# A PEER decoder block: the last gathered chunk's v rows summed on VectorE, some u row products held behind the gate expansion

## The chip, the core and the metric

The kernel runs on one core of one Trainium2 chip. Times are device microseconds (us) of one execution. A core has TensorE (PE in the rows), VectorE (DVE), ScalarE (ACT), GpSimd (POOL) and SyncE (SP), each with its own queue of instructions worked off in order, and 16 DMA engines.

## What is computed

A hybrid block over 1024 tokens plus 16 meta tokens of width 1024: a convolution and a latent attention in parallel, a projection, and then the part that the change touches, an expert mixer with 16384 experts. Per token and head, 16 experts are picked out of 128 x 128 pairs of keys, so 128 experts per token:

```python
        eidx = jnp.take_along_axis(cidx..., sel, axis=-1)
        g = jax.nn.softmax(top_s, axis=-1)
        u = u_tab[eidx]
        act = jax.nn.gelu(jnp.einsum('chkd,cd->chk', u, xb).astype(jnp.float32), approximate=False)
        w = (g * act).astype(xb.dtype)
        return jnp.einsum('chk,chkd->cd', w, v_tab[eidx])
```

The block's input is added, and a last RMS norm gives the output.

## The kernel before, in words

The tokens go in eight chunks of 128. The mixer has two ways of working. Chunks 4 to 7 (DENSE) go through all 16384 experts: `expand` (L741) spreads the gates of a chunk into a full table in DRAM, `g_d`; then `dense` (L801) goes over the 128 first keys i1, in 32 groups of four. For each i1, `dense_u` (L789) multiplies a 128-expert piece of u by the 512 tokens (24 matmuls of 128x512, `pa`), ScalarE takes the Gelu, VectorE multiplies by the gates (L820) and splits the product into a high and a low part (L823, L824); per group the weighted v pieces are summed (96 matmuls, `pv`) and VectorE adds them to `acc` (L837), eight additions per group, 256 in all. Every loaded weight is split into high and low parts by ScalarE and VectorE (L785, L786).

Chunks 0 to 3 (GATHER) fetch only the rows they need. `gather_u` (L679) takes 128 steps j; at each, GpSimd issues an indirect DMA (L690) that brings one u row of 1024 floats per token (512 KB), and VectorE forms the products with the token and their sum (L693, one column of `dots`). Four buffers `ug` hold such rows. When all 128 are there, Gelu and gates make the weights (L695, L696). `gather_v` (L698) then goes by tokens differently: each indirect DMA (L716) brings the 128 v rows of one token, with the experts on the partitions (hence the transposed indices `eT` of `turn`, L659, and the transposed weights), and TensorE sums them over the partitions with 32-column matmuls (L720, 16 for four tokens). Eight buffers `vg` hold such rows.

`gather_all` (L729) chains these: u of chunk 0; then v of chunk 0 beside u of chunk 1; v1 beside u2; v2 beside u3; v3. `dense` takes 1.1 such steps per i1, each of 8 or of 4 rows. This is the order in which the program is written; a scheduler then places the instructions of every engine by its own model, with the written order as priority, so row products of chunk 1 stand as early as the gate expansion, and those of chunk 2 and 3 all along the dense loop. One `xn` buffer serves all chunks, so u1, u2, u3 and what follows them stand in a row.

The expansion of a chunk has four rounds of four passes. A pass makes four VectorE tables of 128x1024 (L755 `two`, L756 `one`, L757 `ah`, L758 `al`; every second `al` is GpSimd's), 16 matmuls, and four ScalarE copies into `st` (L766). A round ends with two stores of 1 MB to `g_d` (L770); three `st` buffers serve two per round, so a round's second half waits for the first store of the round before. The dense loop's first gate load, `gt` (L814), waits for the last rounds' stores.

At the end `finish` (L736) norms each chunk: a ScalarE square and sum (L148), two GpSimd operations (L140, L141), a VectorE product (L738), the store (L739).

Of the kernel before, what the change touches and what calls it, by code (L numbers as in the profile page):

```python
# [4 lines left out]

# [8 lines left out]
F32 = mybir.dt.float32  # L14
# [6 lines left out]
OP = mybir.AluOpType  # L21
# [4 lines left out]
P = 128  # L26
D = 1024
# [35 lines left out]
GATHER = [0, 1, 2, 3]  # L63
# [12 lines left out]
ALP = [1, 3]  # L76
GEB = 6
VB = 8
UB = (4, 3)


@with_exitstack
def trunk_kernel(ctx, tc, x, meta, g_mix, w_ab, w_lat, g_q, w_uq, g_kv, w_ukv, conv_w, conv_b,
                 g_ln, b_ln, g_out, w_out, g_ffn, wq, keys, u_tab, v_tab, u_t, g_fin, cs, out):
    nc = tc.nc
    V, A, G, PE = nc.vector, nc.scalar, nc.gpsimd, nc.tensor
# [16 lines left out]
    h_d = [dram.tile([P, D], F32, name=f"h_d{c}") for c in range(NC)]  # L103
# [25 lines left out]
    def load_bcast(t, ap):  # L129
        nc.sync.dma_start(t, bass.AP(tensor=ap.tensor, offset=ap.offset, ap=[[0, P], [1, t.shape[-1]]]))  # L130
        return t
# [23 lines left out]
    def transpose_to(dst, src, m):  # L155
        PE.transpose(dst, src, ident[:m, :m])
# [448 lines left out]
        V.max_index(i[:, 8:16], v[:, 8:16], s)  # L605

    chunks = [None] * NC
    MTs, tops, weights, picks, kbds = {}, {}, {}, {}, {}

    def select(c, sv, sx):  # L610
# [47 lines left out]

    def turn(c):  # L659

        ef, g = picks[c]
        tp = bank(f"et{c}", (P, 4, P), "s" if c in DENSE else "c")
        transpose_to(tp[:, 0], ef, P)
        eT = const.tile([P, P], I32, name=f"eT{c}", tag="eT", bufs=5)
        V.tensor_copy(eT, tp[:, 0])
        if c in GATHER:
            chunks[c] += (eT,)
        else:
            transpose_to(tp[:, 1], g.rearrange("p h k -> p (h k)"), P)
            t = sel.tile([P, 4, P], F16, name=f"gd{c}", tag="gd", bufs=len(DENSE))  # L670
            A.activation(t[:, 0], tp[:, 1], AF.Copy, scale=GSCALE)
            V.scalar_tensor_tensor(t[:, 1], tp[:, 1], GSCALE, t[:, 0], op0=OP.mult, op1=OP.subtract)
            ii = sel.tile([P, 2, P], I32, name=f"ii{c}", tag="ii", bufs=1)
            V.tensor_scalar(ii[:, 0], eT, 7, None, op0=OP.logical_shift_right)
            V.tensor_scalar(ii[:, 1], eT, NK - 1, None, op0=OP.bitwise_and)
            V.tensor_copy(t[:, 2:4], ii)
            chunks[c] = t

    def gather_u(c):  # L679

        g, ei = chunks[c][:2]
        xn = gu.tile([P, D], F32, name=f"xn{c}", tag="xn", bufs=1)
        nc.sync.dma_start(xn, xn_d[c])
        dots = gu.tile([P, P], F32, name=f"dots{c}", tag="dots", bufs=2)
        weights[c] = dots
        for j in range(P):
            if j and j % 4 == 0:
                yield
            ug = gu.tile([P, D], F32, name=f"ug{c}_{j}", tag="ug", bufs=4)
            G.indirect_dma_start(out=ug, out_offset=None, in_=u_tab,  # L690
                                 in_offset=bass.IndirectOffsetOnAxis(ap=ei[:, j:j + 1], axis=0))
            junk = gu.tile([P, D], BF, name="ujunk", tag="ujunk", bufs=1)
            V.scalar_tensor_tensor(junk, ug, 1.0, xn, op0=OP.mult, op1=OP.mult, accum_out=dots[:, j:j + 1])  # L693
        yield
        A.activation(dots, dots, AF.Gelu)  # L695
        V.tensor_tensor(dots, dots, g.rearrange("p h k -> p (h k)"), op=OP.mult)  # L696

    def gather_v(c):  # L698

# [6 lines left out]
        for q in range(4):  # L706
# [4 lines left out]
            for i in range(8):  # L711
                vg = []
                for j in range(4):
                    t = 32 * j + 8 * q + i
                    vg.append(gp.tile([P, D], F32, name=f"vg{c}_{t}", tag="vg", bufs=VB))
                    G.indirect_dma_start(out=vg[j], out_offset=None, in_=v_tab,  # L716
# [6 lines left out]
                yield  # L723
        ht = gp.tile([P, D], F32, name=f"ht{c}", tag="vg", bufs=VB)
        nc.sync.dma_start(ht, h_d[c])
        V.tensor_tensor(ht, ht, acc, op=OP.add)
        finish(c, ht, load_bcast(gp.tile([P, D], F32, name=f"gfin{c}", tag="vg", bufs=VB), g_fin))

    def gather_all():  # L729
        streams = [gather_u(GATHER[0])]  # L730
        for k in range(len(GATHER) + 1):
            for _ in itertools.zip_longest(*streams):
                yield
            streams = [gather_v(c) for c in GATHER[k:k + 1]] + [gather_u(c) for c in GATHER[k + 1:k + 2]]

    def finish(c, ht, gfin):  # L736
        r = inv_rms(ht, f"o{c}")
        V.scalar_tensor_tensor(ht, ht, r, gfin, op0=OP.mult, op1=OP.mult)  # L738
        nc.scalar.dma_start(out[c * P:(c + 1) * P], ht)  # L739

    def expand(ci):  # L741

        c = DENSE[ci]
        t = chunks[c]
        for q in range(P // TG):
            st = [ex.tile([P, NK // 2, TG], F32, name=f"st{c}_{q}_{i}", tag="st", bufs=STB) for i in range(2)]
            for r0 in range(0, TG, TH):
                sh = [P, TH // 2, NK, 2]

                def col(r):  # L750
                    cv = t[:, r, q * TG + r0:q * TG + r0 + TH].rearrange("p (a b) -> p a b", b=2)
                    return cv[:, :, None, :].broadcast_to(sh)
                one, two, ah, al = [ex.tile(sh, F16, name=f"{n}{c}_{q}_{r0}", tag=n, bufs=b)
                                    for n, b in (("one", 1), ("two", 2), ("ah", 2), ("al", 2))]
                V.tensor_tensor(two, io[:, None].broadcast_to(sh), col(3), op=OP.is_equal)  # L755
                V.tensor_tensor(one, io[:, None].broadcast_to(sh), col(2), op=OP.is_equal)  # L756
                V.tensor_tensor(ah, one, col(0), op=OP.mult)  # L757
                (G if r0 // TH in ALP else V).tensor_tensor(al, one, col(1), op=OP.mult)  # L758
                for r in range(0, TH, 4):
                    pg = bank(f"pg{c}_{q}_{r0}_{r}", (P, 4, NK), "bs"[r // 4 % 2])  # L760
                    for k in range(4):
                        a, b = divmod(r + k, 2)
                        PE.matmul(pg[:, k], two[:, a, :, b], ah[:, a, :, b], start=True, stop=False)  # L763
                        PE.matmul(pg[:, k], two[:, a, :, b], al[:, a, :, b], start=False, stop=True)  # L764
                    for i in range(2):
                        A.activation(st[i][:, :, r0 + r:r0 + r + 4].rearrange("p a b -> p b a"),  # L766
                                     pg[:, :, i * NK // 2:(i + 1) * NK // 2], AF.Copy, scale=1.0 / GSCALE)
            for i in range(2):
                gs = slice(i * NK // 2 // NG, (i + 1) * NK // 2 // NG)
                nc.sync.dma_start(g_d[gs, :, ci * (P // TG) + q].rearrange("g p r -> p g r"),  # L770
                                  st[i].rearrange("p (g a) t -> p g (a t)", a=NG))
# [94 lines left out]
    gu = ctx.enter_context(tc.tile_pool(name="gu", bufs=1, side="right", **RW))  # L866
# [19 lines left out]
    gp = ctx.enter_context(tc.tile_pool(name="gp", bufs=1, side="right", **RW))  # L886
# [98 lines left out]
```

## Time and profile before

| what | value |
|---|---|
| time, median of 3 runs | 3013.92 us (3005.61 to 3018.28) |
| the profiled execution: its own time | 2999.61 us |
| its span, first to last instruction | 2997.8 us |
| busy TensorE, VectorE, ScalarE, GpSimd | 86%, 72%, 34%, 53% |
| mean granted TensorE clock | 0.91 of full speed |
| DMA | 860.44 MB, mean 287 GB/s |

The shares of the whole span mix three kinds of stage, so the rows below are read by stage: the last seven rounds of the gate expansion (1255 to 1391 us from the span's start), the dense loop (first addition to `acc` at 1437, last at 2989), and in it the stretch in which chunk 3's v rows are summed (2626 to 2902). The profiled execution is a little shorter than any of the three timed ones.

### The profile page before, as it was taken

The page shows a single profiled execution, that of the slowest core. Times are in us where ns is not written, and L with a number is a line of the kernel's source. Part 1 is how long each engine was busy: PE and PEld are TensorE (multiplying, and loading weights), DVE is VectorE, ACT ScalarE, POOL GpSimd, SP SyncE. Part 2 cuts the span into 40 slices and gives each one's busy share as a digit, 9 for nine tenths or more (in the row PEclk, how much of TensorE's full clock was granted, in tenths as well). Part 3 has the DMA queues.
Part 4 walks back from the last instruction along what each step waited for, and adds up shares of the span by engine and source line. Part 5 has one row for each costly group of instructions (what it writes and reads, how often), then busy time and mean ns, then how long its engine had stood idle before and what let it go on. Part 6 is the DMA issues. An engine that isn't in the chain of part 4 may idle for free. (4 is left out here: it accounts for less than half of the span.)

```text
span 2997.8 us, 40243 instructions
## 1 busy us (share of the span) xinstructions
PE 2577.1 (86%) x13295; PEld 1932.0 (64%) x13295; DVE 2156.3 (72%) x4749; ACT 1005.9 (34%) x2200; POOL 1579.9 (53%) x1524
## 2 busy tenths in 40 slices
PE   6778758888894764744999999999999999999998
PEld 6675537766662443533887767777777777666666
DVE  4888866999988789997998866565666665533344
ACT  5435425353440332342332223232322222222222
POOL 5885463544658767654344554544454545344420
PEclk9988858998997887856999999999999999999999
DMA  4114789898896998888899999999998989799972
GB/s 141 48 50 129 229 271 318 301 306 285 281 332 233 385 322 272 264 279 306 309 322 318 340 381 340 346 329 344 352 344 329 358 317 362 277 338 332 331 286 74
DMA packets 373138, 860.44 MB, mean 287 GB/s; under 512 B 38016, under 2 KB 134464, under 8 KB 368832
## 3 DMA queue, kind: packets, MB, share of 16 engines
q0 software_dynamic: 147456, 536.94, 50.2%
q1 hardware_dynamic: 217104, 297.77, 29.4%
q10 hardware_dynamic: 8368, 23.15, 2.2%
q8 instruction: 105, 1.72, 0.2%
q14 instruction: 105, 0.86, 0.1%
HBM read 801.02 MB, written 56.71 MB: 286 GB/s over the span
## 5 line engine op out<-in xcount | busy, mean ns | idle before, releaser
L690 POOL DMA_INDIRECT ug<-in_dram,ei x512 | 580.8, 1134 | 662.9 <-DVE ujunk L693 450.9
L716 POOL DMA_INDIRECT vg<-in_dram,eT x512 | 555.6, 1085 | 469.6 <-PE gv L720 332.3
L693 DVE SCALAR_TENSOR_TENSOR ujunk<-ug,xn 128x1024 bf16<-128x1024 f32 x512 | 651.1, 1272 | 70.2 <-DMA ug<-in_dram,ei 67.8
L837 DVE TENSOR_TENSOR acc<-acc,pv 128x512 f32<-128x512 f32 x256 | 171.5, 685 | 251.3 <-PE pv L178 250.8
L720 PE MATMUL gv<-vg,wd 128*32 128x512 f32 x2048 | 266.4, 635 | 12.8 <-DMA vg<-in_dram,eT 12.8
L178 PE MATMUL pv<-v_0h,wh 128*128 128x512 f32 x512 | 201.9, 397 | 18.6 <-ACT wh L823 14.1
L178 PE MATMUL pa<-xdh,u_1l 128*128 128x512 f32 x512 | 203.3, 397 | 5.5 <-DVE u_1l L786 5.5
L178 PE MATMUL pa<-xdh,u_1h 128*128 128x512 f32 x512 | 202.8, 396 | 0.7 <-ACT u_1h L785 0.7
L178 PE MATMUL pa<-xdh,u_0h 128*128 128x512 f32 x512 | 202.4, 395 | 0.8 <-ACT u_0h L785 0.8
L178 PE MATMUL pa<-xdl,u_0h 128*128 128x512 f32 x512 | 201.8, 394 | 0.0
L178 PE MATMUL pa<-xdl,u_1h 128*128 128x512 f32 x512 | 201.7, 394 | 0.0
L178 PE MATMUL pa<-xdh,u_0l 128*128 128x512 f32 x512 | 201.3, 393 | 0.0
L178 PE MATMUL pv<-v_0l,wh 128*128 128x512 f32 x512 | 199.3, 392 | 0.0
L178 PE MATMUL pv<-v_1l,wh 128*128 128x512 f32 x512 | 199.2, 392 | 0.0
L178 PE MATMUL pv<-v_1h,wl 128*128 128x512 f32 x512 | 199.1, 391 | 0.0
L785 ACT ACTIVATE u_1h<-u_1r 128x512 fp32r<-128x512 f32 x128 | 80.7, 631 | 352.5 <-PE pa L178 336.3
L178 PE MATMUL pv<-v_1h,wh 128*128 128x512 f32 x512 | 195.7, 394 | 0.0
L178 PE MATMUL pv<-v_0h,wl 128*128 128x512 f32 x512 | 194.6, 393 | 0.0
L763 PE MATMUL pg<-ah,two 128*128 128x128 f16 x512 | 96.3, 269 | 114.0 <-DVE ah L757 80.6
L766 ACT ACTIVATE st<-pg 128x256 f32<-128x256 f32 x256 | 128.7, 649 | 158.2 <-PE pg L764 122.6
L785 ACT ACTIVATE u_0h<-u_0r 128x512 fp32r<-128x512 f32 x128 | 80.5, 629 | 262.1 <-PE pa L178 251.4
L786 DVE TENSOR_TENSOR u_0l<-u_0r,u_0h 128x512 fp32r<-128x512 f32 x128 | 89.7, 701 | 94.2 <-ACT u_0h L785 89.6
(449 smaller groups left out, 5844.3 us busy)
## 6 DMA issues: line engine op xcount, KB each, us to landing
g_d<-st SPq DMA_DIRECT2D x32, 1024.0 KB
u_0r<-in_dram SPq DMA_DIRECT2D x128, 256.0 KB
u_1r<-in_dram SPq DMA_DIRECT2D x128, 256.0 KB
gt<-g_d SPq DMA_DIRECT2D x32, 1024.0 KB
v_0r<-in_dram SPq DMA_DIRECT2D x128, 256.0 KB
v_1r<-in_dram SPq DMA_DIRECT2D x128, 256.0 KB
wo<-in_dram SPq DMA_DIRECT2D x80, 256.0 KB
wq<-in_dram SPq DMA_DIRECT2D x80, 256.0 KB
```

What stands on the lines that cost most here:

```text
L178: PE.matmul(dst, l, r, start=first and j == 0, stop=last and j == 2)
L690: G.indirect_dma_start(out=ug, out_offset=None, in_=u_tab, in_offset=bass.IndirectOffsetOnAxis(ap=ei[:, j:j + 1], axis=0))
L693: V.scalar_tensor_tensor(junk, ug, 1.0, xn, op0=OP.mult, op1=OP.mult, accum_out=dots[:, j:j + 1])
L716: G.indirect_dma_start(out=vg[j], out_offset=None, in_=v_tab, in_offset=bass.IndirectOffsetOnAxis(ap=eT[:, t:t + 1], axis=0))
L720: PE.matmul(acc[32 * j:32 * j + 32, 512 * n:512 * n + 512], w[:, j, 32 * i:32 * i + 32], vg[j][:, 512 * n:512 * n + 512], start=q == 0 and ...
L763: PE.matmul(pg[:, k], two[:, a, :, b], ah[:, a, :, b], start=True, stop=False)
L766: A.activation(st[i][:, :, r0 + r:r0 + r + 4].rearrange("p a b -> p b a"), pg[:, :, i * NK // 2:(i + 1) * NK // 2], AF.Copy, scale=1.0 / G ...
L785: A.activation(hi, raw, AF.Copy)
L786: V.tensor_tensor(lo, raw, hi.bitcast(F32), op=OP.subtract)
L837: V.tensor_tensor(a, a, pv, op=OP.add)
```

## The change

For the chunks in VROWS (chunk 3) v is gathered as u is: step j brings each token's own j-th v row to its partition, and VectorE multiplies it by the token's weight and adds it to `ht`, which starts as the block's input. The transposed indices, the transposed weights and 512 matmuls of chunk 3 fall away. `ht` takes the `xn` buffer. And the row products of chunk 1 from step 72 on are put behind the last `ah` of the whole expansion in VectorE's queue (`issue_after`).

```diff
+UHOLD = 72
+VROWS = [3]
 def turn(c):
+        if c in VROWS:
+            return
 def gather_u(c):
-            V.scalar_tensor_tensor(junk, ug, 1.0, xn, op0=OP.mult, op1=OP.mult, accum_out=dots[:, j:j + 1])
+            with tc.issue_after(expanded[-1]) if c == GATHER[1] and j >= UHOLD else nullcontext():
+                V.scalar_tensor_tensor(junk, ug, 1.0, xn, op0=OP.mult, op1=OP.mult, accum_out=dots[:, j:j + 1])
+    def gather_v_rows(c):
+        ei = chunks[c][1]
+        ht = gu.tile([P, D], F32, name=f"ht{c}", tag="xn", bufs=1)
+        nc.sync.dma_start(ht, h_d[c])
+        for j in range(P):
+            vg = gp.tile([P, D], F32, name=f"vg{c}_{j}", tag="vg", bufs=VB)
+            G.indirect_dma_start(out=vg, out_offset=None, in_=v_tab,
+                                 in_offset=bass.IndirectOffsetOnAxis(ap=ei[:, j:j + 1], axis=0))
+            V.scalar_tensor_tensor(ht, vg, weights[c][:, j:j + 1], ht, op0=OP.mult, op1=OP.add)
+            if j % 4 == 3:
+                yield
+        finish(c, ht, load_bcast(gp.tile([P, D], F32, name=f"gfin{c}", tag="vg", bufs=VB), g_fin))
 def gather_all():
-            streams = [gather_v(c) for c in GATHER[k:k + 1]] + [gather_u(c) for c in GATHER[k + 1:k + 2]]
+            streams = [(gather_v_rows if c in VROWS else gather_v)(c) for c in GATHER[k:k + 1]] + [gather_u(c) for c in GATHER[k + 1:k + 2]]
 def expand(ci):
-                V.tensor_tensor(ah, one, col(0), op=OP.mult)
+                expanded.append(V.tensor_tensor(ah, one, col(0), op=OP.mult).ins)
```

How the instructions stand after it is shown at three places. First VectorE's queue in the second round of the third chunk's expansion (`ujunk` is a row product of chunk 1, its step is the number behind `ug`; `two`, `one`, `ah`, `al` are the expansion's tables). Before:

```order
L757 TENSOR_TENSOR ah_1_0_9971<-one_1_0_9969,gd_9824 128x1024
L758 TENSOR_TENSOR al_1_0_9972<-one_1_0_9969,gd_9824 128x1024
L756 TENSOR_TENSOR one_1_8_9999<-io,gd_9824 128x1024
L757 TENSOR_TENSOR ah_1_8_10001<-one_1_8_9999,gd_9824 128x1024
L693 SCALAR_TENSOR_TENSOR ujunk,dots_11703<-ug_73_13444,xn_11701 128x1024
L693 SCALAR_TENSOR_TENSOR ujunk,dots_11703<-ug_74_13448,xn_11701 128x1024
L756 TENSOR_TENSOR one_1_16_10029<-io,gd_9824 128x1024
```

With the change (its lines are numbered 21 higher here):

```order
L778 TENSOR_TENSOR ah_1_0_9967<-one_1_0_9965,gd_9820 128x1024
L779 TENSOR_TENSOR al_1_0_9968<-one_1_0_9965,gd_9820 128x1024
L776 TENSOR_TENSOR two_1_8_9996<-io,gd_9820 128x1024
L777 TENSOR_TENSOR one_1_8_9995<-io,gd_9820 128x1024
L778 TENSOR_TENSOR ah_1_8_9997<-one_1_8_9995,gd_9820 128x1024
L776 TENSOR_TENSOR two_1_16_10026<-io,gd_9820 128x1024
```

No row product stands among the last 28 of the 64 passes any more, where 38 stood (steps 72 to 109). The second place is VectorE's queue where the expansion ends, with the change:

```order
L778 TENSOR_TENSOR ah_3_24_10873<-one_3_24_10871,gd_9832 128x1024
L700 SCALAR_TENSOR_TENSOR ujunk,dots_11699<-ug_72_13436,xn_11697 128x1024
L700 SCALAR_TENSOR_TENSOR ujunk,dots_11699<-ug_73_13440,xn_11697 128x1024
L700 SCALAR_TENSOR_TENSOR ujunk,dots_11699<-ug_74_13444,xn_11697 128x1024
L700 SCALAR_TENSOR_TENSOR ujunk,dots_11699<-ug_75_13448,xn_11697 128x1024
```

The held products start here; step 127 of chunk 1 now stands behind 27 of the 256 additions to `acc` (before: behind 7), step 127 of chunk 3 behind 216 (before: 191). The third place is the end of VectorE's queue. Before (`v_3_1l` is a split, `acc<-acc,pv` an addition of the dense loop, the last rows the norms):

```order
L786 TENSOR_TENSOR v_3_1l<-v_3_1r,v_3_1h 128x512
L837 TENSOR_TENSOR acc<-acc,pv_1_0_25895 128x512
L837 TENSOR_TENSOR acc<-acc,pv_1_1_25909 128x512
L837 TENSOR_TENSOR acc<-acc,pv_1_2_25923 128x512
L738 SCALAR_TENSOR_TENSOR acc<-acc,os_25954,gfin 128x1024
L738 SCALAR_TENSOR_TENSOR acc<-acc,os_25961,gfin 128x1024
L837 TENSOR_TENSOR acc<-acc,pv_1_3_25937 128x512
L738 SCALAR_TENSOR_TENSOR acc<-acc,os_25968,gfin 128x1024
```

With the change (`ht<-vg` sums a v row of chunk 3):

```order
L858 TENSOR_TENSOR acc<-acc,pv_1_0_25749 128x512
L714 SCALAR_TENSOR_TENSOR ht_21870<-vg_80_23714,dots_18431,ht_21870 128x1024
L858 TENSOR_TENSOR acc<-acc,pv_1_1_25763 128x512
L858 TENSOR_TENSOR acc<-acc,pv_1_2_25777 128x512
L714 SCALAR_TENSOR_TENSOR ht_21870<-vg_81_23717,dots_18431,ht_21870 128x1024
L858 TENSOR_TENSOR acc<-acc,pv_1_3_25791 128x512
L714 SCALAR_TENSOR_TENSOR ht_21870<-vg_82_23720,dots_18431,ht_21870 128x1024
L714 SCALAR_TENSOR_TENSOR ht_21870<-vg_83_23723,dots_18431,ht_21870 128x1024
```

Of the 128 v rows of chunk 3, 82 (steps 0 to 81) stand ahead of the last addition to `acc`, over the last 20 i1, and 46 (steps 82 to 127) behind it; the five norms stand behind those, and on ScalarE chunk 3's square stands ahead of the squares of chunks 4 to 7.

## Rows read from the trace of the kernel before

**Rows 1.** Busy time of each engine by stretch (us; count of instructions in brackets).

```profile
core 0: us, PE busy (x) PEld busy (x) DVE busy (x) ACT busy (x) POOL busy (x), PEclk, DMA share, GB/s
1255.00:1391.00 136.00, 66.27 (x504) 53.49 (x502) 132.42 (x181) 59.63 (x120) 76.71 (x53) 0.59 0.87 274
...
1437.00:1640.00 203.00, 200.43 (x884) 165.65 (x883) 182.12 (x304) 62.50 (x109) 87.32 (x75) 1.00 0.92 319
1640.00:2626.00 986.00, 981.19 (x4742) 719.20 (x4741) 623.25 (x1024) 276.04 (x473) 479.14 (x439) 1.00 0.92 339
2626.00:2902.00 276.00, 275.78 (x1432) 183.00 (x1431) 101.34 (x159) 66.97 (x111) 121.29 (x125) 1.00 0.93 335
2902.00:2989.00 87.00, 84.52 (x372) 69.33 (x370) 43.22 (x64) 29.67 (x51) 4.63 (x8) 1.00 0.25 82
```

**Rows 2.** Row products (L693) by stretch: VectorE's busy time.

```profile
1255.00:1391.00 136.00, 53.98 (x76) 0.59 0.87 274
```

**Rows 3.** VectorE's groups, 1255 to 1391 (busy us, mean ns | idle before, releaser).

```profile
L693 DVE SCALAR_TENSOR_TENSOR ujunk<-ug,xn 128x1024 bf16<-128x1024 f32 x38 | 53.7, 1412 | 0.0
L757 DVE TENSOR_TENSOR ah<-one,gd 128x1024 f16<-128x1024 f16 x28 | 27.6, 986 | 0.4
```

**Rows 4.** ScalarE's copies into st (L766), busy by stretch.

```profile
1255.00:1391.00 136.00, 55.85 (x112) 0.59 0.87 274
```

**Rows 5.** ScalarE's waits, 1255 to 1391 (us in total, times, longest).

```profile
ACT st L766 <- DMA g_d<-st: 19.3, 4, 7.4
```

**Rows 6.** ScalarE's and VectorE's timelines late in the expansion (start us, us).

```profile
1321.75 1.06 ACT L766 ACTIVATE st<-pg 128x256 f32<-128x256 f32 x2 [2.71 <-DMA g_d<-st]
1388.92 2.37 DVE L757 TENSOR_TENSOR ah<-one,gd 128x1024 f16<-128x1024 f16 x1
...
1422.72 2.50 DVE L820 TENSOR_TENSOR ge<-ge,gt 128x512 f32<-128x512 f32 x4 [8.98 <-DMA gt<-g_d]
```

**Rows 7.** Chunk-sum matmuls (L720) by stretch: TensorE's busy time.

```profile
2626.00:2902.00 276.00, 61.56 (x512) 13.36 (x512) 1.00 0.93 335
```

**Rows 8.** VectorE's groups, 1437 to 1640.

```profile
L693 DVE SCALAR_TENSOR_TENSOR ujunk<-ug,xn 128x1024 bf16<-128x1024 f32 x75 | 91.6, 1221 | 14.8 <-DMA ug<-in_dram,ei 14.3
```

**Rows 9.** VectorE's products of the shape of the new sum, 2626 to 2902.

```profile
L738 DVE SCALAR_TENSOR_TENSOR ht<-ht,os,gfin 128x1024 f32<-128x1024 f32 x1 | 1.3, 1286 | 1.7 <-POOL os L141 1.7
```

**Rows 10.** GpSimd's gathers by group: 1437 to 1640, then 2626 to 2902.

```profile
L690 POOL DMA_INDIRECT ug<-in_dram,ei x75 | 87.7, 1170 | 114.5 <-DVE ujunk L693 100.5 <-DMA ug<-in_dram,ei 6.7 <-issue 4.3
...
L716 POOL DMA_INDIRECT vg<-in_dram,eT x123 | 121.2, 985 | 141.6 <-PE gv L720 107.4 <-issue 20.8 <-PE pv L178 4.6
```

**Rows 11.** GpSimd's timeline, 1433 to 1438.

```profile
1433.20 1.80 POOL L690 DMA_INDIRECT ug<-in_dram,ei  x1 [2.41 <-DVE ujunk L693]
1435.30 0.97 POOL L690 DMA_INDIRECT ug<-in_dram,ei  x1 [0.30 <-issue]
1436.57 0.94 POOL L690 DMA_INDIRECT ug<-in_dram,ei  x1 [0.30 <-issue]
```

**Rows 12.** The page's DMA queues: packets, MB, share of 16 engines' span.

```profile
q0 software_dynamic: 147456, 536.94, 50.2%
```

**Rows 13.** GpSimd's and VectorE's timelines, 1347 to 1352.

```profile
1347.89 2.71 POOL L758 TENSOR_TENSOR al<-one,gd 128x1024 f16<-128x1024 f16 x1 [1.89 <-DVE one L756]
1347.03 0.68 DVE L756 TENSOR_TENSOR one<-io,gd 128x1024 f16<-128x1024 f16 x1
1348.78 2.37 DVE L757 TENSOR_TENSOR ah<-one,gd 128x1024 f16<-128x1024 f16 x1
```

**Rows 14.** VectorE's and ScalarE's timelines at the end.

```profile
2988.41 0.68 DVE L837 TENSOR_TENSOR acc<-acc,pv 128x512 f32<-128x512 f32 x1
2989.20 1.06 ACT L148 ACTIVATE os7j<-acc 128x1024 bf16<-128x1024 f32 x1 [2.45 <-DVE acc L837]
2990.16 0.19 ACT L148 ACTIVATION_READ_ACCUMULATOR os7j<-acc 128x1 f32 x1
2991.28 1.29 DVE L738 SCALAR_TENSOR_TENSOR acc<-acc,os,gfin 128x1024 f32<-128x1024 f32 x1 [1.00 <-POOL os L141]
```

More of the change, by code (lines that the diff above doesn't have):

```diff
@@ L2 @@
 import math
-from contextlib import ExitStack
+from contextlib import ExitStack, nullcontext
 from types import SimpleNamespace
@@ L607, in trunk_kernel @@
     chunks = [None] * NC
+    expanded = []
     MTs, tops, weights, picks, kbds = {}, {}, {}, {}, {}
```

## The prediction

> **What bounds the kernel now.** I read the busy time by stretch first [rows 1], because the shares of the whole span hide that three stages have three limits. From 1255 to 1391, the last seven rounds of the gate expansion, VectorE is busy 132.4 of 136 us and TensorE less than half: VectorE sets the pace. From 1437 to 2902 it is TensorE, 200.4 of 203, 981.2 of 986 and 275.8 of 276 us, at a granted clock of 1.00 (its upper level, 2.4 GHz). The DMA engines are close behind, 0.92 to 0.93 busy. From 2902 to 2989 the gathers are over: DMA falls to 0.25 and GpSimd to 4.6 of 87 us, while the dense loop runs out on TensorE. So before the change the gathers end 87 us ahead of the kernel, and the dense loop ends it: the last addition is over at 2988.41 + 0.68 = 2989.1, and the norms take the 8.7 us to 2997.8 [rows 14].
>
> **The change part by part.**
>
> *Held row products.* In the last 28 passes (7 rounds) stood 38 row products that now stand behind the expansion. They cover 53.98 us of VectorE's time there [rows 2], 1412 ns each with some stretched by a GpSimd table beside them [rows 3]. If VectorE alone counted, the expansion would end 54 us earlier. It doesn't alone count: a round also needs ScalarE's copies, 55.85 / 7 = 8.0 us [rows 4], and its second half waits for the store of the round before. Those waits were 19.3 us in four, 4.8 on average, 7.4 at most [rows 5], although slow rounds gave the stores time. With a wait in every round, a round takes 8.0 + 7.4 = 15.4 or 8.0 + 4.8 = 12.8 us where it took 136 / 7 = 19.4; VectorE's own part is (136 - 54) / 7 = 11.7. So the gain is 7 x 4.0 = 28 to 7 x 6.6 = 46 us by that chain, at most 54, and less if stores take longer than any seen. I take 37, the middle of the chain's two values. From the last `ah` to the first gate product 34 us pass [rows 6], set by the last stores and the gate load; I keep them. The first held products fit in there: ten stand ahead of the first gate product in the new order, at about 2 us each.
>
> *What the held products do later.* Chunk 1's 46 late products (before, steps 72 to 117 stood ahead of the loop's splits) now go into the dense loop, and u1, u2, u3 and v3 stand in a row, so everything in that row moves back. VectorE has room: 623 of 986 us busy in the long middle [rows 1]. In the fullest stretch, 75 row products in 203 us with 182 busy, TensorE still lost only 2.6 us [rows 1, 8]. What hides this work is TensorE's own pace; if it were gone, 46 products of 1.22 us would be 56 us. I charge nothing here, because the new order gives the first 28 i1 about as many products as the old one did (16 to each 3 to 5 i1), only from an earlier place in the row.
>
> *The matmuls removed.* 512 matmuls of chunk 3, 61.6 us of TensorE's time [rows 7], in the stage where TensorE is never idle: all of it comes off the dense loop, if nothing else steps in. VectorE in that stage is busy 101 of 276 us; now it gets 82 row sums over 20 i1. A sum has the shape of the product that took 1286 ns [rows 9], so 82 x 1.29 = 106 us. That is a stage about as full as the one from 1437 to 1640, and I charge the 3 us that TensorE lost there. The DMA engines move the same bytes; they are given 82 rows in the last 20 i1 where before 128 rows went into the same number of i1, so they don't become the limit ahead of the last addition.
>
> *The tail.* This is the price. 46 sums stand behind the last addition, and the end waits for them: the DVE queue holds the norms behind them, too. The rate of such a row is bounded by three things. VectorE: 1.29 us [rows 9]. GpSimd: 0.985 us for a gather with VectorE free of row products, 1.170 beside them [rows 10], and 0.30 between two [rows 11], so 1.29 to 1.47. DMA: the gather queue took 50.2% of 16 engines for 1024 rows [rows 12], 0.502 x 2997.8 / 1024 = 1.47 us a row, with other loads beside it. The low end is 1.29. The high end is what chunk 3's rows took before, 276 / 128 = 2.16 us [rows 1]. I take 1.47, since GpSimd's rate beside row products and the queue's mean give the same: 46 x 1.47 = 68 us. (Up to eight rows are already there when the tail begins, and the last one has to land; I let the two cancel.)
>
> A row speaks against part of this price. A GpSimd table and VectorE do block each other: beside an `al` of 2.71 us an `ah` took 2.37 us where such a table takes 0.68 [rows 13]. A gather that started beside row products took 1.80 us, and those right behind it 0.97 and 0.94 with row products still running [rows 11]; so here the gathers are delayed now and then, 0.19 us on average. The Trainium skill, SBUF — State Buffer, section "SBUF: two separate sides", has a stricter rule: VectorE and GpSimd share a port pair under an exclusive lock, taken also by a VectorE operation with two SBUF inputs against a GpSimd operation that reads SBUF, and the loser waits for the whole operation. By that rule the two would alternate in the tail, and the sum would be about +25 us, where the rows on the gathers make it -23; the rows on the `al` agree with the rule, those on the gathers mostly don't.
>
> *The end.* Before, one square (1.06 + 0.19 us) stood between the last addition and the norm [rows 14]; now chunk 3's square goes first and four follow, so 4 x 1.25 = 5 us more.
>
> *The rest.* One transpose of indices, one of weights and a few small VectorE operations fall away: under a us each, counted at nothing.
>
> **Sum:** -37 - 61.6 + 3 + 68 + 5 = -23 us. The profiled execution took 2999.6 us, so it would be 2977; it lies 14 us below the median of the timed runs, 3013.9, and for those I say 2991. A measurement of this kernel can tell a difference of about 0.5%, 15 us, from none.
>
> **The rivals.**
>
> *Tail in lock-step (slower).* In the tail VectorE does nothing but row sums, so every gather meets one. If the sum (1.29 us) and the gather (0.94 us, plus 0.30) take turns, a row takes 2.53 us and the tail 116: -37 - 61.6 + 3 + 116 + 5 = +25, 3039. It decides from 1.97 us a row on, where the sum is zero, and 2.3 us is where it can be told. For it: the `al` rows [rows 13]; against it: the two gathers of 0.95 us among row products [rows 11] and the mean of 1.17 [rows 10]. Chance 0.13.
>
> *The stores take over the expansion (same).* The chain of copy, store and copy was hidden behind VectorE; if a round takes 17.5 us or more, because stores and weight loads bunch up when the rounds come faster, the gain there is under 13 us: +1 or so, 3015. For it: the four waits [rows 5], the first at 1321.75 [rows 6], so all in the second half of the stretch. Against it: 20 MB of row gathers leave this stretch, which had the DMA engines at 0.87 [rows 1]. Chance 0.25.
>
> *Both sides better (faster still).* VectorE alone counts in the expansion (-54), and the tail runs at VectorE's 1.29 us (59): -54 - 61.6 + 3 + 59 + 5 = -49, 2965. For it: row gathers no longer compete with the stores, and no other load competes in the tail. Against it: ScalarE's waits [rows 5]. Chance 0.2.
>
> *The rows don't leave TensorE faster.* If a v row lands late, the splits behind its sum in VectorE's queue wait, and TensorE with them; then the 61.6 us shrink. In the fullest stretch VectorE waited 14.3 us for 75 rows with four buffers [rows 8] and TensorE lost 2.6; with eight buffers and fewer rows per us I hold it for a part of the range, not for a case (0.02).
>
> **How the numbers follow.** The forecast has 0.4. Range: the low end is the faster rival, 2965, less a few us for the scatter of medians, 2961. The high end goes to the forecast with the slow chain (28 instead of 37) and a tail row of 1.9 us (87 instead of 68), +5, 3019, and a few us of scatter: 3023; the lock-step case lies mostly above it. Faster by over 0.5% (below 2999): nearly all of the faster rival and some 0.37 of the forecast's 0.4, 0.57. Slower by over 0.5%: 0.12 out of the lock-step rival and a little of the others, 0.13. Within: 0.30.
>
> **What would show it.** In the changed kernel's profile: the first addition to `acc` some 37 us earlier; the time from the first to the last addition some 59 us shorter; then 46 row sums on VectorE with TensorE idle, about 68 us, ending in five norms. Wrong would be a first addition at the old time (stores), TensorE with gaps in the last 20 i1 (late rows), or a tail of more than 90 us.

## The result and the profile after

The changed kernel takes 2976.5 us (median of 4 runs, 2974.5 to 2979.0) against 3011.7 us before (4 runs, 3005.6 to 3018.3): a ratio of 0.9883 [0.9859, 0.9907], 35 us faster. The forecast was 2991 in a range of 2961 to 3023. The profiled execution took 2974.46 us, its span is 2972.7, against 2999.61 and 2997.8 before; so the two traces differ by 25 us and the medians by 35. Two more profiles, below, say most of why.

Busy time by stretch of the changed kernel: the second half of the expansion, the way to the first addition, four pieces that are the dense loop and the tail, and the end. It answers to [rows 1].

```profile
core 0: us, PE busy (x) PEld busy (x) DVE busy (x) ACT busy (x) POOL busy (x), PEclk, DMA share, GB/s
1275.00:1362.00 87.00, 55.85 (x437) 45.17 (x438) 82.81 (x99) 53.52 (x111) 31.47 (x15) 0.56 0.69 197
1362.00:1413.00 51.00, 32.91 (x143) 26.57 (x141) 30.86 (x49) 14.29 (x28) 18.18 (x15) 0.75 0.90 320
1413.00:1616.00 203.00, 200.22 (x875) 164.80 (x873) 180.39 (x304) 63.46 (x111) 88.40 (x76) 0.99 0.90 318
1616.00:2600.00 984.00, 978.85 (x4737) 720.93 (x4738) 632.77 (x1039) 273.69 (x471) 474.96 (x447) 1.00 0.94 344
2600.00:2895.00 295.00, 293.73 (x1301) 240.91 (x1299) 263.27 (x350) 90.41 (x156) 148.05 (x114) 1.00 0.89 311
2895.00:2957.00 62.00, 0.00 (x0) 0.00 (x0) 59.19 (x47) 0.13 (x1) 40.25 (x39) 0.51 0.93 358
2957.00:2973.00 16.00, 0.00 (x0) 0.00 (x0) 6.43 (x5) 5.62 (x10) 7.20 (x10) 0.50 0.40 164
```

The stretch from the 37th `ah` to the last (27 of the last 28 passes; the expectations below count from nought and call it the 36th) lasted 127.2 us before and lasts 87.4, and VectorE is still busy 82.8 of 87. VectorE's timelines give the first `ah` of the expansion, the 37th and the first addition to `acc`, before:

```profile
974.93 0.67 DVE L757 TENSOR_TENSOR ah<-one,gd 128x1024 f16<-128x1024 f16 x1
...
1261.70 0.68 DVE L757 TENSOR_TENSOR ah<-one,gd 128x1024 f16<-128x1024 f16 x1
...
1436.78 0.69 DVE L837 TENSOR_TENSOR acc<-acc,pv 128x512 f32<-128x512 f32 x1 [0.68 <-PE pv L178]
```

And after, with the last `ah` too (before it started at 1388.92, [rows 6]):

```profile
977.85 0.68 DVE L778 TENSOR_TENSOR ah<-one,gd 128x1024 f16<-128x1024 f16 x1
...
1274.78 0.69 DVE L778 TENSOR_TENSOR ah<-one,gd 128x1024 f16<-128x1024 f16 x1
...
1362.21 0.69 DVE L778 TENSOR_TENSOR ah<-one,gd 128x1024 f16<-128x1024 f16 x1
...
1412.48 0.69 DVE L858 TENSOR_TENSOR acc<-acc,pv 128x512 f32<-128x512 f32 x1 [0.80 <-PE pv L181]
```

The loop keeps TensorE as full as before (293.7 of 295 at its end). Then stand 62 us in which TensorE has nothing and VectorE is busy 59.2.

VectorE's timeline around the last addition, one of GpSimd's gathers in the tail, then VectorE's and ScalarE's timelines from the last sum on (start us, us); they answer to [rows 14].

```profile
2894.49 0.68 DVE L858 TENSOR_TENSOR acc<-acc,pv 128x512 f32<-128x512 f32 x1
2895.09 5.24 DVE L714 SCALAR_TENSOR_TENSOR ht<-vg,dots,ht 128x1024 f32<-128x1024 f32 x4
...
2900.13 1.02 POOL L712 DMA_INDIRECT vg<-in_dram,ei  x1 [0.30 <-issue]
...
2955.55 1.28 DVE L714 SCALAR_TENSOR_TENSOR ht<-vg,dots,ht 128x1024 f32<-128x1024 f32 x1 [1.07 <-DMA vg<-in_dram,ei]
2956.87 1.06 ACT L151 ACTIVATE os3j<-ht 128x1024 bf16<-128x1024 f32 x1 [73.88 <-DVE ht L714]
...
2966.14 1.29 DVE L759 SCALAR_TENSOR_TENSOR acc<-acc,os,gfin 128x1024 f32<-128x1024 f32 x1 [0.44 <-POOL os L144]
```

GpSimd's and VectorE's groups in the tail, 2895 to 2957; they answer to [rows 9, 10].

```profile
L712 POOL DMA_INDIRECT vg<-in_dram,ei x39 | 40.4, 1036 | 13.6 <-issue 11.3 <-DVE ht L714 2.3
...
L714 DVE SCALAR_TENSOR_TENSOR ht<-vg,dots,ht 128x1024 f32<-128x1024 f32 x46 | 59.1, 1285 | 2.6 <-DMA vg<-in_dram,ei 1.1
```

ScalarE's waits from 1275 to 1362 (us in total, times, longest); they answer to [rows 5].

```profile
ACT st L787 <- DMA g_d<-st: 11.9, 4, 3.1
```

Where the time went, by the two traces: the first addition came at 1412.5 instead of 1436.8 (-24.3); from first to last addition 1482.0 instead of 1551.6 us passed (-69.6); behind the last addition's start stand 78.2 instead of 9.4 us (+68.8). Sum -25.1.

### The profile page after: what moved, and what is told of

Read it like the earlier page. It is cut to its first block, busy times and chain, and to the rows that moved or that the text cites. A ratio compares the mean times of both kernels' runs of the same rounds, so it can differ in the third digit from the quotient of the medians.

```text
span 2972.7 us, 39531 instructions
## 1 busy us (share of the span) xinstructions
PE 2507.0 (84%) x12781; PEld 1925.3 (65%) x12781; DVE 2310.2 (78%) x4866; ACT 1001.3 (34%) x2200; POOL 1599.3 (54%) x1524
## 3 DMA queue, kind: packets, MB, share of 16 engines
q0 software_dynamic: 147456, 536.94, 50.3%
## 4 chain that ended last, share of the span: by engine, by line
PE 47%; DVE 21%; issue 11%; DMA 9%; POOL 7%; ACT 2%; another core or an unknown queue 0%; POOLq 0%; DVEq 0%; SPq 0%; ACTq 0%
PE pv L181 18%; PE pa L181 17%; PE gv L741 5%; DVE ujunk L700 4%; DMA ug<-in_dram,ei 4%; POOL vg L712 3%; DMA g_d<-st 2%; DVE acc L315 1%; POOL ug L696 1%; PE q L587 1%; DVE eq L642 1%; DVE ef L645 1%; DVE ah L778 1%; PE op L567 1%; DVE sx L605 1%
## 5 line engine op out<-in xcount | busy, mean ns | idle before, releaser
L696 POOL DMA_INDIRECT ug<-in_dram,ei x512 | 565.6, 1105 | 731.3 <-DVE ujunk L700 518.9
L737 POOL DMA_INDIRECT vg<-in_dram,eT x384 | 416.5, 1085 | 286.8 <-PE gv L741 181.2
L712 POOL DMA_INDIRECT vg<-in_dram,ei x128 | 161.2, 1260 | 103.8 <-DVE ht L714 81.5
L741 PE MATMUL gv<-vg,wd 128*32 128x512 f32 x1536 | 197.8, 631 | 15.0 <-DMA vg<-in_dram,eT 15.0
```

The lines of the kernel that those rows point to most:

```text
L696: G.indirect_dma_start(out=ug, out_offset=None, in_=u_tab, in_offset=bass.IndirectOffsetOnAxis(ap=ei[:, j:j + 1], axis=0))
L712: G.indirect_dma_start(out=vg, out_offset=None, in_=v_tab, in_offset=bass.IndirectOffsetOnAxis(ap=ei[:, j:j + 1], axis=0))
L741: PE.matmul(acc[32 * j:32 * j + 32, 512 * n:512 * n + 512], w[:, j, 32 * i:32 * i + 32], vg[j][:, 512 * n:512 * n + 512], start=q == 0 and ...
```

## The experiments

The theory to be tested: the terms are independent, and rows come in one chain (u1, u2, u3, v3) that ends some way ahead of the loop before. Both parts of the change draw on that distance. What the two are worth alone should then add up to more than both together. The rivals stand with the runs. The first four kernels ran beside eleven runs of the kernel before (median 3011.5), the next four beside eleven others (3012.5). Of each stretch the columns are those of the table above.

**Row sums alone.**

```diff
-UHOLD = 72
+UHOLD = 128
```

> The row sums of chunk 3 alone; no product is held behind the expansion. Theory (independent terms, and a row chain u1, u2, u3, v3 that runs one after the other, so that every held product comes back as a row sum behind the last addition): the expansion and the first addition stand as in the kernel before (first addition near 1437 us), the dense loop from first to last addition is as short as in the changed kernel, about 1482 us instead of 1552, and only 3 sums are left behind the last addition, 4 us instead of 62, with the end at 16 us instead of 9. So 3012 - 70 + 4 + 7 = 2953 us, some 23 us faster than the changed kernel: the held products would then cost more in the tail than they save in the expansion. Rival (the two parts need each other): with the products back in the expansion nothing else is gained, the rows of chunk 3 come into the last i1 too early or too late for TensorE, and the loop loses what the tail no longer has: 2976 us or more, with gaps of TensorE in the last 32 i1.

Measured: 2950.5 us, ratio 0.9804 [0.9776, 0.9832]. First addition 1443.1, loop 1477.9, three sums behind it, 20.4 us from the last addition to the end. Its first `ah` and first addition, the three sums as one row of VectorE's timeline, then its loop in two stretches, and the tail:

```profile
972.94 0.68 DVE L778 TENSOR_TENSOR ah<-one,gd 128x1024 f16<-128x1024 f16 x1
...
1443.10 0.69 DVE L858 TENSOR_TENSOR acc<-acc,pv 128x512 f32<-128x512 f32 x1 [0.17 <-PE pv L181]
...
2921.63 3.92 DVE L714 SCALAR_TENSOR_TENSOR ht<-vg,dots,ht 128x1024 f32<-128x1024 f32 x3
...
1443.00:2600.00 1157.00, 1153.34 (x5493) 865.78 (x5495) 794.50 (x1308) 330.47 (x568) 552.28 (x506) 1.00 0.93 339
2600.00:2921.00 321.00, 320.26 (x1428) 260.96 (x1420) 294.13 (x354) 98.39 (x169) 174.79 (x134) 1.00 0.92 329
2921.00:2926.00 5.00, 0.00 (x0) 0.00 (x0) 4.48 (x5) 0.41 (x1) 0.00 (x0) 0.88 0.00 0
```

The rival falls: TensorE has no gaps (320.3 of 321 us). Without the held products the change is 26 us better than with them. By the traces: the held products bring the first addition forward by 30.6 us (1443.1 to 1412.5), add 4.1 to the loop, and add 57.8 behind it (20.4 to 78.2); 31 us lost.

**Held products alone.**

```diff
-VROWS = [3]
+VROWS = []
```

> The held products alone; the v rows of chunk 3 are summed by TensorE as before. Theory: the first addition comes 24 us earlier, as in the changed kernel (1412 us), the dense loop keeps its 1552 us, because the 46 rows that are pushed back take 46 x 1.3 to 1.5 = 60 to 69 us out of the 87 us by which the gathers ended ahead of the kernel before, and the end keeps its 9 us: 3012 - 24 = 2988 us, no tail of rows on VectorE. Rival (late rows): the last rows land after TensorE has nothing else left, the dense loop grows by 15 us or more, and the time is 3000 us or above, no gain at all. The changed kernel's gain would in the first case be less than the sum of its parts by just the tail (-24 and -59 against -35).

Measured: 2983.8 us, 0.9916 [0.9892, 0.9940], 28 us faster. First addition 1413.3, loop 1545.4, but 22.6 us at the end, since the last rows are late after all. VectorE's timeline at the first `ah` and the first addition, and TensorE's at the end:

```profile
986.05 0.67 DVE L778 TENSOR_TENSOR ah<-one,gd 128x1024 f16<-128x1024 f16 x1
...
1413.26 0.68 DVE L858 TENSOR_TENSOR acc<-acc,pv 128x512 f32<-128x512 f32 x1
...
2954.58 0.39 PE L181 MATMUL pv<-v_1l,wh 128*128 128x512 f32 x1
2954.90 1.92 PE L741 MATMUL gv<-vg,wd 128*32 128x512 f32 x16
2956.75 0.50 PE L181 MATMUL pv<-v_1h,wl 128*128 128x512 f32 x1
...
2961.62 2.59 PE L741 MATMUL gv<-vg,wd 128*32 128x512 f32 x16 [2.96 <-DMA vg<-in_dram,eT]
```

The last group of four rows waits 2.96 us for its data behind the loop's last matmul. So the theory holds with a piece of the rival in it: the last gather, 101 us ahead of the last addition before (2887.7 and 2988.4), is now 4.5 us ahead (2954.2 and 2958.7). The two parts alone add to -61 - 28 = -89 us, and together they are worth -35: 54 us are lost between them, and the tail of both together is 43 sums x 1.32 = 57 us longer than that of row sums alone.

The rows show a term of the prediction as well. The loop's matmuls start 0.23 us apart; around the group of 16, which is 1.92 us busy, 2956.75 - 2954.58 = 2.17 us pass between two of them, 1.94 more than a step, and the next step, to the matmul at 2957.09, is 0.11 longer as well. So this group cost TensorE 2.05 us. The 512 removed matmuls are 32 groups, 66 us, and the last 32 i1 became 69.4 us shorter (397.3 to 327.9). The other 4 us weren't traced to anything.

**Two accumulators.**

```diff
+        h2 = gu.tile([P, D], F32, name=f"h2{c}", tag="ug", bufs=4)
...
-            V.scalar_tensor_tensor(ht, vg, weights[c][:, j:j + 1], ht, op0=OP.mult, op1=OP.add)
+            if j == 0:
+                V.tensor_scalar(h2, vg, weights[c][:, j:j + 1], None, op0=OP.mult)
+            else:
+                a = (h2, ht)[j % 2]
+                V.scalar_tensor_tensor(a, vg, weights[c][:, j:j + 1], a, op0=OP.mult, op1=OP.add)
...
+        V.tensor_tensor(ht, ht, h2, op=OP.add)
```

> The changed kernel with two accumulators for the row sums of chunk 3, taken in turn, and one addition more at the end; the order puts about 27 of the 46 sums ahead of the last addition, so 19 are left behind it. Two questions. What sets the 1.32 us between two sums in the tail: if it is that each sum needs the one before (the sum itself is 1.29 us), the distance falls to 1.25 us or less; if it is the gathers of GpSimd (1.02 us and 0.30 between two), it stays at 1.32. And is it VectorE's place in the order or the row chain that makes the tail: if the chain of rows (gathers one after the other) makes it, the 27 sums that stand earlier wait for their rows, TensorE waits with them in the last i1, and the time stays at 2976 us within 6; if it is only the place, the tail shrinks by 27 x 1.32 = 36 us and the time is near 2941.

Measured: 2968.2 us, 0.9866 [0.9838, 0.9894], 8 us below the changed kernel; but the two intervals overlap, so the times alone don't tell the two apart. The expectation miscounted: the 19 were the sums of one of the two accumulators, and 37 stand behind the last addition, so only 9 moved ahead of it. Of VectorE's timeline in that tail:

```profile
2911.41 1.29 DVE L719 SCALAR_TENSOR_TENSOR h<-vg,dots,h 128x1024 f32<-128x1024 f32 x1
2912.61 1.30 DVE L719 SCALAR_TENSOR_TENSOR ht<-vg,dots,ht 128x1024 f32<-128x1024 f32 x1
2913.98 1.28 DVE L719 SCALAR_TENSOR_TENSOR h<-vg,dots,h 128x1024 f32<-128x1024 f32 x1
```

GpSimd's gathers in the same tail:

```profile
2911.40 0.95 POOL L713 DMA_INDIRECT vg<-in_dram,ei  x1 [0.30 <-DVE ht L719]
2912.65 0.95 POOL L713 DMA_INDIRECT vg<-in_dram,ei  x1 [0.30 <-issue]
```

Sums now start 1.19 to 1.37 us apart, 1.25 in the mean of the first 34 distances, where in the changed kernel each distance but the last (2.36) was 1.31 or 1.32. So that a sum needs the one before it costs 0.07 us a row. The run of row sums alone shows that 1.32 is VectorE's own pace on one accumulator: its three sums start (3.92 - 1.28) / 2 = 1.32 apart, and GpSimd is busy 0.00 us beside them. Gathers take 0.95 + 0.30 = 1.25 us here and leave GpSimd no time: they set the pace now. In the changed kernel a gather in the tail takes 1.02 + 0.30 = 1.32, so both engines were full there; how VectorE's dependence reaches the gather's length is not shown. The 9 sums and the shorter distance took 11.9 us off the stretch behind the last addition (78.2 to 66.3) and put 3.6 on the loop: so their place in the order counted, and the rows came in time for most of that. As 9 moved where 27 were meant, the run says no more on that question.

**Row sums for chunks 2 and 3**, no product held (the sum of chunk 2 lies in one of the eight `vg` buffers).

```diff
-VROWS = [3]
+VROWS = [2, 3]
```

> The row sums on VectorE for chunk 2 as well as chunk 3, and no product held. Theory by TensorE's time: another 512 matmuls off the loop, another 69 us, but 23 sums are left behind the last addition: 3012 - 139 + 23 x 1.32 + 7 = 2910 us. Rival (VectorE or the DMA engines become the bound): in the i1 in which the row sums of chunk 2 stand beside the products of chunk 3 VectorE has four of each for every two i1 or so and is over 0.95 busy, the loop takes its pace from there, the 69 us shrink to 30 or less, and the time is 2945 us or more.

Measured: 2905.4 us, 0.9654 [0.9627, 0.9682], 71 us faster than the changed kernel and the fastest of all. First addition 1437.1, loop 1422.7 (129 less than before, where 139 were expected), 23 sums behind it. The second row below is a part of the first:

```profile
1437.00:2600.00 1163.00, 1151.31 (x5263) 900.27 (x5262) 953.30 (x1456) 342.92 (x597) 591.22 (x514) 1.00 0.94 346
2157.00:2600.00 443.00, 435.83 (x1903) 355.22 (x1902) 429.04 (x591) 135.93 (x241) 247.69 (x201) 1.00 0.96 356
2600.00:2860.00 260.00, 259.03 (x1141) 213.62 (x1139) 246.74 (x298) 80.77 (x139) 137.54 (x107) 1.00 0.91 324
2860.00:2890.00 30.00, 0.00 (x0) 0.00 (x0) 29.21 (x24) 0.00 (x0) 17.03 (x16) 0.57 0.91 339
```

TensorE is still the loop's bound, with some 12 us of gaps in 1163. Seven of them lie from 2157 to 2600, where VectorE is busy 429 of 443 us and the DMA engines 0.96: the rival comes near there.

**Chunks 1 to 3, and all four** (the sums of all chunks but chunk 3 in `vg` buffers, as in the run before).

```diff
-VROWS = [2, 3]
+VROWS = [1, 2, 3]
```

> Row sums on VectorE for chunks 1, 2 and 3, no product held. In the order 88 sums stand behind the last addition where rows23 had 23. Theory of the row chain (rows can't come faster than the DMA engines, 0.95 busy in that part of rows23, so the loop outruns its rows): the loop loses another 55 to 60 us, the tail grows by 65 x 1.32 = 86 us, and the time is rows23's 2905 + 26 to 31 = about 2933 us. Rival (TensorE's time is still what counts, and the tail's rows come faster): 2905 or less.

```diff
-VROWS = [1, 2, 3]
+VROWS = [0, 1, 2, 3]
```

> The same for all four chunks. Chunk 0's row sums then stand in the gate expansion: 246 row operations between the first table of the expansion and the first addition, where rows23 has 90, but 3 sums are left behind the last addition. If VectorE sets the expansion's pace: it was 407 of 450 us busy there in rows23, and 156 operations of 1.3 us are 203 us more, so the first addition comes about 160 us later (203 less the 43 us that were free); the loop loses three chunks' 69 us at the most against the kernel before, 1552 - 207 = 1345; sum 1437 + 160 + 1345 + 4 + 16 = 2962 us in the profile, slower than rows23. Rival (the expansion has other work to wait for, and the row sums fit beside it): the first addition comes less than 80 us later, and the time is below 2885 us.

Measured: three chunks 2928.6 us, 0.9720 [0.9704, 0.9737]; four 2996.8 us, 0.9960 [0.9944, 0.9976]. With three the loop is 1335.8 us, 87 less than with two (55 to 60 were expected), the first addition 20 us later, and 88 sums stand behind the last addition; the time is only 4 us off, because the two misses, in the loop and at the first addition, mostly cancel. VectorE's group of row sums in the tail of the three:

```profile
L714 DVE SCALAR_TENSOR_TENSOR ht<-vg,dots,ht 128x1024 f32<-128x1024 f32 x88 | 113.1, 1285 | 5.2 <-DMA vg<-in_dram,ei 2.1
```

The stretches of the four, from the first `ah` to the loop's end:

```profile
1005.00:1390.00 385.00, 151.66 (x878) 120.73 (x877) 381.78 (x792) 100.49 (x201) 250.85 (x190) 0.61 0.76 256
1390.00:1562.00 172.00, 53.22 (x432) 43.90 (x432) 170.08 (x205) 55.94 (x111) 133.96 (x93) 0.50 0.96 334
1562.00:1626.00 64.00, 32.14 (x131) 26.01 (x132) 48.29 (x60) 11.98 (x22) 37.22 (x29) 0.70 1.00 383
1626.00:2973.00 1347.00, 1339.31 (x5887) 1104.63 (x5885) 1274.01 (x1786) 418.91 (x736) 731.28 (x560) 1.00 0.93 338
```

With four, VectorE is busy 381.8 of 385 and 170.1 of 172 us of the expansion, and the first addition comes at 1626.3, 189 later than with two (160 were expected); the loop's 1346 is the 1345 of the expectation. So the same edit saves where TensorE is the bound and costs where VectorE is. The profiled execution took 2995 us where 2962 were expected. 29 us of that are in the expansion: its first `ah` came 18 us later (1004.9, with two 986.5), 21 us of VectorE's time stayed free that were meant to be filled, and the added work was 193 us instead of 203.

**Is it VectorE's time that shortens the expansion?** Two runs of the kernel before. The first leaves out 46 row products of chunk 1 and keeps their gathers:

```diff
-            V.scalar_tensor_tensor(junk, ug, 1.0, xn, op0=OP.mult, op1=OP.mult, accum_out=dots[:, j:j + 1])
+            if c == GATHER[1] and 72 <= j < 118:
+                V.tensor_copy(dots[:, j:j + 1], ug[:, 0:1])
+            else:
+                V.scalar_tensor_tensor(junk, ug, 1.0, xn, op0=OP.mult, op1=OP.mult, accum_out=dots[:, j:j + 1])
```

> The kernel before, with the 46 row products of chunk 1 from the 72nd on left out (a copy of one column stands for each, so the gathers and the buffers stay as they are). What made the expansion shorter in the changed kernel, VectorE's time or the gathers that moved with the products? If VectorE's time: the stretch from the 36th first table of a pass (ah) to the last falls from 127 us to 85 to 95, as in the changed kernel (87), though all gathers are still there, and the first addition comes 30 to 42 us earlier. If the DMA engines: the stretch stays above 115 us.

Measured: 2973.4 us, one execution. The stretch took 97 us and the first addition came at 1408.3, 28.5 earlier. Each is 2 us outside what VectorE's time was to give, and the stretch is far from the 115 of the other theory. (Counted from the first `ah`, the first addition came after 430.0 us, 32 to 34 earlier than in the two profiles of the kernel before.) Of the gathers 28 stand in the stretch, where 36 stood in the 127 us before: as many per us. VectorE's waits in the stretch (us in total, times, longest), first here, then all of them in the changed kernel:

```profile
DVE one L779 <- POOL al L781: 9.0, 4, 2.8
...
DVE two L776 <- PE pg L785: 3.0, 3, 2.1
```

GpSimd's tables, which stand in one queue with the gathers, come late here, 9.0 us in four waits; in the changed kernel, where the gathers moved too, VectorE waits for none of them. Of the 40 us gained some 30 are VectorE's time. The other 10 aren't all GpSimd's: with held products alone (above), where products and gathers moved and no row is summed on VectorE, the stretch takes 93.9 us (1270.95 to 1364.86), 3 less than here, with 3.6 us of waits for GpSimd's tables. The last 6.5 us came only with the row sums, and were not traced.

The second run keeps the products and leaves out the 46 gathers (the products take an old row):

```diff
-            ug = gu.tile([P, D], F32, name=f"ug{c}_{j}", tag="ug", bufs=4)
-            G.indirect_dma_start(out=ug, out_offset=None, in_=u_tab,
-                                 in_offset=bass.IndirectOffsetOnAxis(ap=ei[:, j:j + 1], axis=0))
+            if not (c == GATHER[1] and 72 <= j < 118):
+                ug = gu.tile([P, D], F32, name=f"ug{c}_{j}", tag="ug", bufs=4)
+                G.indirect_dma_start(out=ug, out_offset=None, in_=u_tab,
+                                     in_offset=bass.IndirectOffsetOnAxis(ap=ei[:, j:j + 1], axis=0))
```

> The counterpart: the kernel before, in which the same 46 products are made, but on the row that was gathered last ahead of them, so 46 gathers of chunk 1 are left out and VectorE's work is the same. If VectorE's time sets the stretch it stays near 127 us (120 to 130); if the gathers' share of the DMA engines or of GpSimd's time does, it falls below 100 us.

Measured: 3035.0 us, one execution: slower. The stretch took 142 us, with 52 products in it where the kernel before had 37, since without gathers the order put nearly all of the 46 there. Two of its stretches:

```profile
1270.00:1362.00 92.00, 46.90 (x332) 37.11 (x330) 91.85 (x134) 39.32 (x80) 21.50 (x11) 0.63 0.46 134
1362.00:1390.00 28.00, 9.70 (x80) 8.11 (x80) 28.00 (x40) 10.37 (x21) 6.40 (x3) 0.50 0.28 76
```

VectorE's group of products, 1255 to 1426:

```profile
L702 DVE SCALAR_TENSOR_TENSOR ujunk<-ug,xn 128x1024 bf16<-128x1024 f32 x58 | 90.2, 1556 | 0.0
```

The DMA engines are at 0.28 to 0.46, and VectorE is busy 91.85 of 92 and 28.00 of 28 us. Fewer products made the stretch shorter, fewer gathers did not: VectorE's time sets it. The 120 to 130 us of the expectation were missed because the number of products there didn't stay the same.

**Both kernels once more**, for a second profile of each.

> The kernel before, unchanged, for a second profile: its first profiled execution was 12 us shorter than the median of its timed runs, the changed kernel's 2 us shorter, and that is why the two traces differ by 25 us and the medians by 35. If the scatter lies ahead of the dense loop, first to last addition takes 1551.6 us again within 3, and what the execution is longer or shorter by stands in the time of the first addition (1436.8 in the first profile, later by the difference here). If it lies in the loop, the first addition stands at 1437 within 3, and the loop's time carries it.

> The changed kernel, unchanged, for the same reason. If the scatter lies ahead of the dense loop: first to last addition 1482 us within 3, 46 sums behind it at 1.32 us each again, and the first addition carries the difference to 2974. If it lies in the loop or the tail, one of these moves.

Measured: 3008.9 and 2978.5 us. The first table of the expansion (the first `ah`) came at 987.2 instead of 974.9 before the change, and at 985.7 instead of 977.9 after it; the last stretch of the expansion took 127.2 us again, and 88.2 (87.4 in the first profile). The loop took 1546.4 (1551.6) and 1480.3 us (1482.0), with 46 sums at 1.32 us behind it again. So most of the scatter, up to 12 us, lies ahead of the expansion, and 5 us in the loop, 2 more than expected. The first profile of the kernel before was one with an early start.

## Why the prediction was right, and where it was off

Its mechanism held: the expansion got shorter by VectorE's time, the loop by TensorE's, and the tail took back a part. That its sum came so near is partly luck (the last point). Step by step, with the two profiles of each kernel:

- **Held row products, -37.** The stretch became 39.8 us shorter: a round takes 12.9 us on average (87.4 us are 27 passes, 6.75 rounds) and 12.3 in the last whole ones, near the 12.8 that was the chain's lower value. At the first addition less arrived. Counted from the first `ah`, which leaves the scatter ahead of it out, it comes after 461.9 and 464.1 us before and 434.6 and 433.4 after: -29. The rest went into the passes ahead of the stretch: from the first `ah` to the 37th 287 and 289 us passed before, 297 and 295 after. That is not the held products' doing. By the same count the first addition comes after 427.2 us with held products alone and after 470.2 with row sums alone, and the 37th `ah` after 285 and 294. So the held products give 36 us with the row sums (470.2 against 434) and without (463 against 427.2), nearly the 37; and the row sums cost 7 us ahead of the loop, where the prediction put what else they change at nothing (*The rest*). The two parts alone were profiled once each; why the row sums cost this was not traced. What follows the last table was nearly kept, as it said: 47.9 us from the last `ah` to the first addition before, 50.3 after.
- **Stores as the bound** (rival, 0.25): didn't come. Four waits of 11.9 us in all, 3.1 the longest, against [rows 5].
- **What the held products do later, 0.** Right: the first 96 i1 take 1154.1 us, before 1154.3 (in the second pair 1152.5 and 1149.3).
- **The matmuls removed, -61.6, and +3 for VectorE.** -69.6 in the first pair of profiles, -66.1 in the second (-69.4 and -69.3 in the last 32 i1 alone). The term was the busy time of 512 matmuls; some 0.13 us around each of 32 groups came on top, 4 us stay open, and VectorE's fuller stretch cost nothing that can be told.
- **The tail, 46 x 1.47 = 68.** 46 sums it was, at 1.32, 61 us. The price was too high because GpSimd's gather takes 1.04 us among row sums and not 1.17, and the queue's mean row over the whole span [rows 12] was no measure of a row in the tail.
- **The tail in lock-step** (rival, 0.13): didn't come. In 46 sums one behind the other, with 2.6 us idle between them, 39 gathers took 1036 ns on average, and only one of them (1.87 us) more than 1.02; the Trainium skill's rule on the shared port pair (SBUF — State Buffer, section "SBUF: two separate sides"), which would have made them take turns, is not what these rows show for gathers. For GpSimd's tables the run without gathers shows it once more (below).
- **Both sides better** (rival, 0.2): half of it came. The tail ran at 1.32 us a row, near the 1.29 of one sum, but the expansion kept more than VectorE's time alone. **Rows that don't leave TensorE faster** (0.02): didn't come, TensorE is busy 293.7 of the loop's last 295 us.
- **The end, +5.** 15.9 us from the last sum on, before 8.7: +7.
- **The step to the medians, +14.** This is where the forecast's own error comes from. The sum gave 2977 for a profiled execution, and it took 2974; the 14 us were added because the one profile of the kernel before lay that much under its median, as if that were a part of the kernel. It was one early start: in the second profile the first `ah` comes 12 us later. The changed kernel's median lies 2 us above its profile, and so the forecast came out 15 us high.
- **The sum itself** is nearer than its terms. In the first pair of profiles the way to the first addition gained 24 us where 37 were forecast, the loop 70 where 59 were, and the part behind the last addition cost 69 where 73 were: misses of +13, -11 and -4. In the second pair they are +5, -7 and -5. That they largely cancel is luck.

What the prediction had without making use of it: by its own terms a held product gives 37 / 46 = 0.8 us and a sum in the tail costs 1.47. Measured, it is 36 / 46 = 0.8 and 1.32, so this half of the change loses where it stands beside the other half. For the row sums alone its terms make -61.6 + 3 + 3 x 1.47 + 5 = -49, 2950 us for a profiled execution, which took 2943; what it did not have is that only 3 sums are left behind the last addition without held products.

Open: the medians of the two kernels differ by 35 us, the means of two profiles each by 28 (3002.5 and 2974.8 us of span); the rest may be scatter, which these runs don't settle.

## What to carry to other kernels

Where a chain of small steps runs beside the engine that bounds a loop, note how far ahead of the loop it ends: that distance is a budget, and both a shorter loop and a step put off draw on it. Here one part alone nearly spent it (the last gather 101 us ahead of the last addition before, 4.5 with held products alone), and with both each step put off cost its full price at the end. Price the two ends of a deferral against each other (here 0.8 us gained, 1.32 paid) before putting it beside another gain. And take the step from a profile to a median from several profiled executions, or leave it out.

## What was not expected of the hardware

A row sum's record is 1.28 us long, but on two accumulators in turn the next one can start after 1.20 us, and on one it starts after 1.32.

Without gathers beside them the row products of the expansion took longer, 1556 ns instead of 1412 [rows 3]. GpSimd's and VectorE's timelines in that run:

```profile
1319.86 2.19 POOL L781 TENSOR_TENSOR al<-one,gd 128x1024 f16<-128x1024 f16 x1 [7.76 <-DVE one L779]
...
1317.87 1.21 DVE L702 SCALAR_TENSOR_TENSOR ujunk<-ug,xn 128x1024 bf16<-128x1024 f32 x1
...
1320.22 2.91 DVE L702 SCALAR_TENSOR_TENSOR ujunk<-ug,xn 128x1024 bf16<-128x1024 f32 x1
```

Of these 58 products 11 took 2.91 to 3.38 us, and all 11 overlap a GpSimd table; the others took 1.21 to 1.25, five that overlap a table among them. In the kernel before 4 of 38 were stretched, each beside a table, and 18 that ran beside a gather and no table took 1.21 or 1.22. So it is the tables that stretch the products, not the gathers; without gathers a larger share of them was stretched, and why was not traced.
